# Query-key products on half of the array's rows: three 64-row products per head, two heads side by side

## The chip, the cores and the metric

The kernel runs on one core of a Trainium2 chip. The metric is the device time of one execution in microseconds (us); the comparison is between medians of several runs. TensorE is called PE in the rows of the profile (PEld is its weight load), VectorE is DVE, ScalarE is ACT, GpSimd is POOL, and SyncE, which here issues nearly all DMAs, is SP.

## The reference

One encoder block on x of shape (1, 1024, 1024) in float32. A single projection gives q, k, v and a gate z for two groups of eight heads of width 64. Group A is neighbourhood attention on a 16 by 64 grid of tokens (window 8 by 16, a learned bias per head and offset); group B is windowed attention (|i - j| <= 128) with rotary positions, four query heads per key head, and a sink logit. Both are gated and projected back:

```python
h = jnp.einsum('bsd,de->bse', x, w_in[layer])
q_a, k_a, v_a, z_a, q_b, k_b, v_b, z_b = jnp.split(h, SPLIT_POINTS, axis=-1)
y_a = neighborhood_attention(q_a, k_a, v_a, rel_pos_bias[layer])   # softmax(q k / 8 + bias) v
qb, kb = rotary(q_b, positions), rotary(k_b, positions)
y_b = windowed_gqa_with_sink(qb, kb, v_b, sink_logits[layer])      # softmax([q k / 8, sink]) v
mixed = jnp.concatenate([y_a * jax.nn.silu(z_a), y_b * jax.nn.silu(z_b)], axis=-1)
y = jnp.einsum('bse,ed->bsd', mixed, w_out[layer])
x = layer_norm(DEEPNORM_ALPHA * x + y, ln_gain[layer], ln_bias[layer])
```

## The kernel before

**Numbers in two halves.** Matmuls run in float16. Each operand is split into a high part and a low part (the remainder), and a product is the sum of three: high by high, low by high, high by low.

**Projection.** `project` makes one 128-column piece of h (two heads of q, k or z), in two halves of 512 tokens, each half being 24 matmuls of 512 columns (line 411) into one of two accumulator banks `ps_pj`. `evac` empties the bank: for z by a tanh and a product, for q and k by `split_q` and `split_k`, which write float16 high and low parts to tiles `qs` and `ks`. ScalarE makes the high part (lines 287, 289), VectorE or GpSimd the low part (293, 295). Before the change each head has a tile of its own. In a `q` tile one head's high part fills its own 64 partitions and its low part the other 64; in the `kh` tile the key's high part stands in both halves, where GpSimd copies it (`dup_`, line 325). So one matmul over 128 partitions (line 934) gives two of the three products at once, and one over 64 partitions (line 938) gives the third. For the group B keys `kb` GpSimd copies the low part as well, since heads of either half use it.

**Units.** The attention is 128 units of 128 queries by up to 384 keys: first 64 of group B (`p`, token block, head `j` of the pair), then 64 of group A (`p`, column block `b`, row `half`, head `j`). Four units make a quad, whose query-key products are issued together by `batch` and `stage_mm`. In group B the quad's units are (j=0, j=1) of one block and then of the next; in group A they are (half 0, j 0), (half 1, j 1), (half 0, j 1), (half 1, j 0).

**One unit's chain.** The product lands in one of five banks `ps_s`. VectorE adds the mask or the bias and takes the row minimum of the negated score (`stage_qk`, line 963, result in `sn` and `nm`). ScalarE takes the exponential (`stage_exp`, line 980), which goes back to the bank, or for the third unit of each quad to a tile `px`. `stage_tr` makes the high part on ScalarE (line 990) and the low part on VectorE (line 991, which frees the bank), and SyncE issues a transposing DMA (line 994). The product with v follows some nine steps later (`stage_pv`, line 1022, in the single bank `ps_t`), then the division by the sum (`stage_on`, lines 1027 and 1029), a transpose on PE (`stage_ot`, line 1040) and the product with the gate (lines 1046 and 1050), which reads `ps_t`.

**The order.** Everything from the projections to the last unit is issued in an order written out by hand: one step `i` per unit. In step `i` VectorE gets the minimum of unit `i`, then the low part of unit `i - 1`; ScalarE gets the high part of `i - 1`, then the exponential of `i`; when `i % 4 == 3` the next quad's products follow. Between these, `pump_to` feeds PE with matmuls of the list `fill`: the projections of `FILL`, and at the end the first terms of the output projection (`out_head`, matmuls of line 1170). Small jobs of the other engines wait in `queues` and are taken a few per step by `pop`. After the last step `final` issues the rest of the output projection and the layer norm; there a scheduler sets the order, and it may also put such work between the rows written by hand.

Of the kernel before, what the change touches and what calls it, by code (L numbers as in the profile page):

```python
# [18 lines left out]
GW = 64  # L19
# [34 lines left out]
EO = (4, 5, 6, 7, 0, 1, 2, 3)  # L54
# [9 lines left out]
NROW = (11, 12)  # L64
# [7 lines left out]
def hybrid_block(ctx, tc, xT, x, wt, wv, wo, bias, sink, gain, lbias, cos, sin, bmask, out):  # L72
# [203 lines left out]

    stks = {}

    def own(kind, p, j):
        if (kind, p, j) not in stks:  # L280
            stks[kind, p, j] = stk(kind)
        return stks[kind, p, j]

    def split_hl(h, l, src, scaled, eng):
        def hi():
            if scaled:
                nc.scalar.activation(h(), src, AF.Copy, scale=QSCALE)
            else:
                nc.scalar.copy(h(), src)

        def lo():
            if scaled:
                nc.vector.scalar_tensor_tensor(l(), src, QSCALE, h(), op0=ALU.mult, op1=ALU.subtract)
            else:
                (nc.gpsimd if eng == "pool" else nc.vector).tensor_sub(l(), src, h())

        return hi, lo

    def split_q(p, half, src, dep=None):
        sl = slice(512 * half, 512 * half + 512)  # L300
        ops = []
        prio = 0 if dep is None else 1
        eng = "pool" if dep and clock["step"] is not None else "dve"
        for j in range(2):
            a, o = slice(64 * j, 64 * j + 64), slice(64 - 64 * j, 128 - 64 * j)
            hi, lo = split_hl(lambda j=j, a=a: own("q", p, j)[a, sl], lambda j=j, o=o: own("q", p, j)[o, sl],
                              src[a], dep is None, eng)
            o1 = enq("act", hi, dep, prio=prio, after=28 if dep else 0)
            ops.append(enq(eng, lo, o1, prio=prio, after=32 if dep else 0))
            stk_ops.setdefault((p, j, half), []).append(ops[-1])  # L310
        return ops

    def split_k(p, half, src, dep=None):
        sl = slice(512 * half, 512 * half + 512)
        ops = []
        prio = 0 if dep is None else 1
        eng = "pool" if dep and clock["step"] is not None else "dve"
        for j in range(2):
            a, o = slice(64 * j, 64 * j + 64), slice(64 - 64 * j, 128 - 64 * j)
            hi, lo = split_hl(lambda j=j, a=a: own("kh", p, j)[a, sl], lambda j=j, a=a: own("kl", p, j)[a, sl],  # L320
                              src[a], dep is None, eng)

            def dup_(w, j=j, a=a, o=o):
                t = own(w, p, j)
                nc.gpsimd.tensor_copy(t[o, sl], t[a, sl])

            o1 = enq("act", hi, dep, prio=prio, after=28 if dep else 0)
            o2 = enq(eng, lo, o1, prio=prio, after=32 if dep else 0)
            ops.append(o2)
            dup = [enq("pool", lambda d=dup_: d("kh"), o1, after=32 if dep else 0)]  # L330
            dup.append(enq("pool", lambda d=dup_: d("kl"), o2, after=36) if dep else o2)
            stk_ops.setdefault((p, j, half), []).extend(dup)
        return ops

    def rope(ps, half):
        live = clock["step"] is not None
# [11 lines left out]
    def evac(name, half, ps):  # L348
        sl = slice(512 * half, 512 * half + 512)
        kind = name.rstrip("0123")  # L350
        p = int(name[-1]) if name[-1].isdigit() else 0
        n = ORDER.index(name)
        if kind in ("kb", "qb"):
            raw, o1, o5 = rope(ps, half)
            if kind == "kb":
                split_k("b", half, raw, o5)
            else:
                split_q(f"b{p}", half, raw, o5)
            return [o1]
        if kind == "k":  # L360
            return split_k(p, half, ps)
        if kind == "q":
            return split_q(p, half, ps)
# [7 lines left out]
        o = enq("act", lambda: nc.scalar.activation(zt[e][:, sl], ps, AF.Tanh, scale=half_inv), prio=0)  # L371
        o2 = enq("dve", lambda: nc.vector.scalar_tensor_tensor(
            zt[e][:, sl], zt[e][:, sl], 1.0, ps, op0=ALU.add, op1=ALU.mult), o, prio=0)
        stk_ops.setdefault(name, []).append(o2)
        return [o2]
# [7 lines left out]
    def new_group():  # L383
        if len(groups) >= 2:
            need(*groups[-2])
        return bank("pj")
# [527 lines left out]

    def qk_parts(u):
        g, p, j, t = u
        n, _c = geom(u)
        if g == "a":
            b, half = t
            q = stks["q", p, j][:, 512 * half + 128 * b:512 * half + 128 * b + 128]  # L920
            sl = [stks[w, p, j].rearrange("p (r c) -> p r c", c=GW)[
                :, 4 * half:4 * half + NROW[half], WIN0[b]:WIN0[b] + WINW[b]] for w in ("kh", "kl")]
            return NROW[half] * WINW[b], q, sl
        q = stks["q", f"b{p}", j][:, 128 * t:128 * t + 128]
        lo = max(t - 1, 0) * 128
        return n, q, [stks[w, "b", p // 2][:, lo:lo + n] for w in ("kh", "kl")]

    def stage_mm(us):
        for u in us:
            m, q, sl = qk_parts(u)  # L930
            ps = st[u, "ps"] = bank("s")
            if units.index(u) == WO_MAX + 4:
                wo_turn(ps)
            nc.tensor.matmul(ps[:, :m], q, sl[0], start=True, stop=False)  # L934
        for u in us:
            m, q, sl = qk_parts(u)
            a = slice(64 * u[2], 64 * u[2] + 64)
            nc.tensor.matmul(st[u, "ps"][:, :m], q[a], sl[1][a], start=False, stop=True)  # L938

    def stage_qk(u):  # L940
        g, p, j, t = u
# [231 lines left out]

    obank = {}

    def out_head(ts, es, tag):
        for t in ts:
            if tag == "pj":
                obank[t, 0] = new_group()
                groups.append([])  # L1180
            elif tag is not None:
                obank[t, 0] = bank(tag)
        for e in es:
            for t in ts:
                yield from out_mms(t, 0, obank[t, 0], [e])

    def final():
        actx.close()
# [116 lines left out]
        with tc.manual_schedule():  # L1305
# [11 lines left out]
    def batch(n):  # L1317
        us = units[n:n + 4]
        for u in us:
            if u[3] in (0, 4):  # L1320
                need(*stk_ops[f"b{u[1]}", u[2], u[3] // 4])
            if u[0] == "a" and n % 16 == 0:
                need(*stk_ops[u[1], u[2], 0], *stk_ops[u[1], u[2], 1])
        stage_mm(us)

    OT_AT = {(q, 0): (q - 3,) for q in range(3, 30)}
# [4 lines left out]
    for i in range(-LD, NU + LO):  # L1331
# [151 lines left out]
```

## Time and profile before

| | us |
|---|---|
| median of three runs (448.36 to 448.79) | 448.76 |
| the profiled execution: its own time | 448.48 |
| its span, from the first to the last instruction | 446.7 |
| PE busy, in the span | 437.7 |
| VectorE, ScalarE, GpSimd busy | 348.1, 310.9, 225.6 |

PE's granted clock is full (0.999). A busy share counts an instruction from its start to its modelled end; neighbouring matmuls overlap, so a matmul row of 379 ns is not the distance to the next one, and a short wait of PE can be hidden under the end of the matmul before it. Distances between starts show such waits.

### The profile page before, as it was taken

To read this page: it belongs to the slowest core of one execution; us is meant where nothing else is said; L and a number is where in the kernel's file an instruction comes from. 1 tells how busy PE (TensorE), PEld (TensorE's weight loads), DVE (VectorE), ACT (ScalarE), POOL (GpSimd) and SP (SyncE) were. 2 spreads that over 40 slices of the span, in tenths; PEclk is the share of its full clock that TensorE was granted. 3 is DMA by queue.
4 is the path that set the end of the run, shared out by engine and by line. 5 is a ranking of instruction groups with operands and counts; after the bars stand their busy time and mean duration, and the time that the engine had idled before them with its cause. 6 is when DMAs were issued, how large, how long until landed. Compare 5 with 4: busy or idle time off the path is not lost.

```text
span 446.7 us, 9468 instructions
## 1 busy us (share of the span) xinstructions
PE 437.7 (98%) x3275; PEld 241.9 (54%) x3275; DVE 348.1 (78%) x851; ACT 310.9 (70%) x721; POOL 225.6 (51%) x226
## 2 busy tenths in 40 slices
PE   9999999999999999999999999999999999999994
PEld 8987754444444545554545555555554554444442
DVE  5999948739978888888898798898877736179954
ACT  6798269766688889798898888888877866002211
POOL 0206734556837658768326529647563455005740
PEclk9999999999999999999999999999999999999999
DMA  8992078986837879577799879999999877101721
GB/s 299 302 361 70 21 248 261 306 272 257 287 91 179 132 165 179 131 131 159 154 170 197 177 168 197 199 200 202 217 213 197 154 185 320 48 0 70 251 79 70
DMA packets 133983, 81.76 MB, mean 183 GB/s; under 512 B 101296, under 2 KB 113328, under 8 KB 133680
## 3 DMA queue, kind: packets, MB, share of 16 engines
q1 hardware_dynamic: 133504, 80.67, 73.8%
q8 instruction: 25, 0.41, 0.4%
q10 hardware_dynamic: 432, 0.49, 0.4%
q14 instruction: 22, 0.18, 0.2%
HBM read 50.73 MB, written 9.96 MB: 136 GB/s over the span
## 4 chain that ended last, share of the span: by engine, by line
PE 69%; issue 9%; DVE 9%; ACT 6%; POOL 5%; DMA 1%; POOLq 0%; DVEq 0%; ACTq 0%
PE ps_pj L411 26%; PE ps_s L1170 11%; PE ps_t L1022 6%; PE ps_pj L1170 5%; PE ps_s L688 4%; PE ps_s L634 4%; PE ps_s L934 3%; POOL wl L217 2%; PE ps_t L1170 2%; PE ps_s L938 2%; ACT ps_s L980 2%; PE ps_pj L634 2%; PE ps_t L1040 2%; POOL wr L216 2%; DVE sn L963 2%
## 5 line engine op out<-in xcount | busy, mean ns | idle before, releaser
L411 PE MATMUL ps_pj<-xf,wh 128*128 128x512 f16 x672 | 204.0, 379 | 0.0
L411 PE MATMUL ps_pj<-xf,wl 128*128 128x512 f16 x336 | 127.6, 380 | 0.0
L411 PEld LDWEIGHTS <-wh 128*128 128x128 f16 x672 | 64.9, 98 | 72.6 <-issue 2.7
L980 ACT ACTIVATE ps_s<-sn,nm 128x385 f32<-128x385 f32 (+3 forms) x96 | 52.4, 546 | 19.9 <-DVE nm L963 18.7
L1170 PEld LDWEIGHTS <-m 128*128 128x128 f16 x408 | 38.8, 98 | 44.3 <-DVE eps L1191 1.2
L991 DVE SCALAR_TENSOR_TENSOR split<-ps_s,split 128x384 f16<-128x384 f32 (+2 forms) x96 | 49.1, 511 | 12.6 <-ACT split L990 12.2
L411 PEld LDWEIGHTS <-wl 128*128 128x128 f16 x336 | 32.8, 98 | 39.9 <-issue 6.2
L1170 PE MATMUL ps_s<-wo,m 128*128 128x512 f16 (+1 forms) x240 | 53.5, 374 | 0.0
L216 POOL TENSOR_SCALAR wr<-wr,wsc 128x512 f32<-128x512 f32 x26 | 22.0, 847 | 45.7 <-ACT wh L211 39.4
L990 ACT ACTIVATE split<-ps_s 128x384 f16<-128x384 f32 (+2 forms) x96 | 43.3, 451 | 2.0
L963 DVE CUSTOM_DVE_ANT_0 sn<-ps_s,bm,nsk 128x384 f32<-128x384 f32 (+1 forms) x64 | 40.6, 635 | 0.2
L1022 PEld LDWEIGHTS <-tr 128*128 128x128 f16 (+1 forms) x1104 | 36.6, 98 | 7.6
L963 DVE CUSTOM_DVE_ANT_0 sn<-ps_s,bias,sg 128x264 f32<-128x264 f32 (+1 forms) x64 | 35.0, 547 | 2.6 <-PE ps_s L938 1.9
L217 POOL TENSOR_TENSOR wl<-wr,wh 128x512 f16<-128x512 f32 x26 | 32.1, 1234 | 2.2
L1227 ACT ACTIVATE sd<-mv,eps 128x1 f32<-128x1 f32 x8 | 2.4, 294 | 43.7 <-DVE mv L1225 41.4
L908 POOL TENSOR_SCALAR bias<-bias,rsg 128x552 f32<-128x552 f32 (+1 forms) x24 | 18.7, 779 | 26.7 <-DMA bias<-in_bias 23.7
L1269 POOL TENSOR_TENSOR xr<-xr,gb 128x512 f32<-128x512 f32 x7 | 11.2, 1606 | 40.6 <-ACT xr L1266 40.6
L934 PE MATMUL ps_s<-ks,qs 128*128 128x384 f16 (+4 forms) x128 | 24.6, 306 | 1.3 <-DVE split L991 0.8
L991 DVE SCALAR_TENSOR_TENSOR split<-px,split 128x384 f16<-128x384 f32 (+2 forms) x32 | 23.2, 724 | 3.3 <-ACT split L990 3.2
L688 PEld LDWEIGHTS <-xf 128*128 128x128 f16 x216 | 21.0, 98 | 8.4 <-DVE xf L542 0.3
L1170 PE MATMUL ps_pj<-wo,m 128*128 128x512 f16 (+1 forms) x120 | 24.4, 347 | 0.0
L688 PE MATMUL ps_s<-wf,xf 128*128 128x320 f16 x144 | 23.8, 299 | 0.0
(216 smaller groups left out, 841.9 us busy)
## 6 DMA issues: line engine op xcount, KB each, us to landing
ws<-in_wt SPq DMA_DIRECT2D x15, 512.0 KB, 5.6
wr<-in_wt SPq DMA_DIRECT2D x26, 256.0 KB, 3.0
bias<-in_bias SPq DMA_DIRECT2D x16, 276.0 KB, 3.3
wor<-in_wo SPq DMA_DIRECT2D x16, 256.0 KB, 3.4
xr<-in_x SPq DMA_DIRECT2D x8, 512.0 KB, 7.6
xraw<-in_xT SPq DMA_DIRECT2D x15, 256.0 KB, 5.2
out<-xr SPq DMA_DIRECT2D x14, 256.0 KB, 2.0
bias<-in_bias SPq DMA_DIRECT2D x8, 368.0 KB, 4.4
```

The source lines that it names most:

```text
L216: nc.gpsimd.tensor_scalar(raw, raw, scale, 1.0, op0=ALU.mult, op1=ALU.mult)
L217: nc.gpsimd.tensor_sub(l, raw, h)
L411: nc.tensor.matmul(ps, a[:, k % 4, :], mv, start=(k == 0 and i == 0), stop=(k == KT - 1 and i == 2))
L634: nc.tensor.matmul(banks[t, a][:, :320], lh[k][:, 128 * t:128 * t + 128], rh[k][:, 320 * a:320 * a + 320], start=(k == 0 and i == 0), stop ...
L688: nc.tensor.matmul(ps[:, :320], lh[t // 4, k][:, 128 * (t % 4):128 * (t % 4) + 128], rh[k][:, 320 * a:320 * a + 320], start=(k == first an ...
L934: nc.tensor.matmul(ps[:, :m], q, sl[0], start=True, stop=False)
L963: nc.vector.tensor_tensor_reduce(sn[:, :m], ps[:, :m], bias_t, sg[:, c:c + 1], init, op0=ALU.add, op1=ALU.min, accum_out=nm)
L980: nc.scalar.activation(pt[:, :m], sn[:, :m], AF.Exp, bias=nm, scale=-1.0, accum_out=sm[:, k:k + 1])
L990: nc.scalar.activation(hl[:, :m, 0, :c], src, AF.Copy, scale=PSCALE)
L991: nc.vector.scalar_tensor_tensor(hl[:, :m, 1, :c], src, PSCALE, hl[:, :m, 0, :c], op0=ALU.mult, op1=ALU.subtract)
L1022: nc.tensor.matmul(ps[:, o:o + HD], a, b_, start=(i == 0), stop=(i == len(mms) - 1))
L1170: nc.tensor.matmul(ps, lh[:, ts], rh[:, cs], start=(e == EO[0] and i == 0), stop=(e == EO[-1] and i == 2))
```

## The change

- **Tiles.** `own` no longer keeps a tile per head. The high parts of both heads of a pair stand in one tile (head 0 in partitions 0 to 63, head 1 in 64 to 127), the low parts in another. `split_pair` writes each with one instruction over 128 partitions where `split_q` and `split_k` used two over 64. The copies on GpSimd stay for the group B keys alone (`split_kb`).
- **Products.** Each unit gets three matmuls over the 64 partitions of its head. They are issued in pairs, one head of each half in turn: (0, 1) and (2, 3) of the quad in group B, (0, 2) and (3, 1) in group A.
- **VectorE's order.** In step `i` it gets the minimum of unit `i + 1`. For the first unit of a quad this is right behind the quad's products, at the end of the step before.
- **Output projection.** The first twelve terms of (rows 0, second half) and (rows 1, second half) move from `final` to the end of `fill`, so they come after the last unit's transposes in the order written by hand.

```diff
-    def own(kind, p, j):
+    def own(kind, p):
...
+    def split_pair(kinds, p, half, src, dep=None):
         sl = slice(512 * half, 512 * half + 512)
-        ops = []
         prio = 0 if dep is None else 1
         eng = "pool" if dep and clock["step"] is not None else "dve"
+        hi, lo = split_hl(lambda: own(kinds[0], p)[:, sl], lambda: own(kinds[1], p)[:, sl], src, dep is None, eng)
+        o1 = enq("act", hi, dep, prio=prio, after=28 if dep else 0)
+        o2 = enq(eng, lo, o1, prio=prio, after=32 if dep else 0)
+        stk_ops.setdefault((p, half), []).append(o2)
+        return [o2]
...
     def qk_parts(u):
         g, p, j, t = u
-        n, _c = geom(u)
+        r = slice(64 * j, 64 * j + 64)
         if g == "a":
             b, half = t
+            n, o = NROW[half] * WINW[b], 512 * half + 128 * b
+            q = [stks[w, p][r, o:o + 128] for w in ("qh", "ql")]
+            k = [stks[w, p].rearrange("p (r c) -> p r c", c=GW)[
+                r, 4 * half:4 * half + NROW[half], WIN0[b]:WIN0[b] + WINW[b]] for w in ("kh", "kl")]
...
+        return n, ((q[0], k[0]), (q[1], k[0]), (q[0], k[1]))
 
     def stage_mm(us):
         for u in us:
-            m, q, sl = qk_parts(u)
             ps = st[u, "ps"] = bank("s")
             if units.index(u) == WO_MAX + 4:
                 wo_turn(ps)
-            nc.tensor.matmul(ps[:, :m], q, sl[0], start=True, stop=False)
-        for u in us:
-            m, q, sl = qk_parts(u)
-            a = slice(64 * u[2], 64 * u[2] + 64)
-            nc.tensor.matmul(st[u, "ps"][:, :m], q[a], sl[1][a], start=False, stop=True)
+        for pair in ((0, 1), (2, 3)) if us[0][0] == "b" else ((0, 2), (3, 1)):
+            for i in range(3):
+                for u in (us[c] for c in pair):
+                    m, parts = qk_parts(u)
+                    nc.tensor.matmul(st[u, "ps"][:, :m], *parts[i], start=i == 0, stop=i == 2)
...
-        for t, tag in ((0, "s"), (1, "s"), (2, "t")):
+        for t, tag in ((2, "t"),):
             obank[t, 1] = bank(tag)
             list(out_mms(t, 1, obank[t, 1], EO[:4]))
...
-                 out_head((3, 4), EO[:4], "s")))
+                 out_head((3, 4), EO[:4], "s"), out_head((0,), EO[:4], "s", 1), out_head((1,), EO[:4], "s", 1)))
...
         if i < NU:
             if i == 0:
                 batch(0)
-            stage_qk(units[i])
+                stage_qk(units[0])
+            if i % 4 != 3:
+                stage_qk(units[i + 1])
...
         if i % 4 == 3 and i + 1 < NU:
             pump_to(i + QK_AT)
             batch(i + 1)
+            stage_qk(units[i + 1])
```

On PE, the last quad (group A). Before: four matmuls over 128 partitions, of which the last two stand here, then four over 64; `ks_4442` and `ks_4471` are the doubled high parts of two heads' keys, `ks_4460` and `ks_4476` their low parts.

```order
L934 MATMUL ps_s_5346<-ks_4471,qs_4729 128x264
L934 LDWEIGHTS qs_4701
L934 MATMUL ps_s_5348<-ks_4442,qs_4701 128x288
L938 LDWEIGHTS qs_4701
L938 MATMUL ps_s_5342<-ks_4460,qs_4701 128x264
L938 LDWEIGHTS qs_4729
L938 MATMUL ps_s_5344<-ks_4476,qs_4729 128x288
L938 LDWEIGHTS qs_4729
L938 MATMUL ps_s_5346<-ks_4476,qs_4729 128x264
L938 LDWEIGHTS qs_4701
L938 MATMUL ps_s_5348<-ks_4460,qs_4701 128x288
```

The same quad now, its second pair of units: six matmuls over 64 partitions; `qs_4739` holds the high parts of both heads' queries, `qs_4763` the low ones, `ks_4483` and `ks_4507` the keys' high and low parts.

```order
L930 LDWEIGHTS qs_4739
L930 MATMUL ps_s_5397<-ks_4483,qs_4739 128x288
L930 LDWEIGHTS qs_4739
L930 MATMUL ps_s_5395<-ks_4483,qs_4739 128x288
L930 LDWEIGHTS qs_4763
L930 MATMUL ps_s_5397<-ks_4483,qs_4763 128x288
L930 LDWEIGHTS qs_4763
L930 MATMUL ps_s_5395<-ks_4483,qs_4763 128x288
L930 LDWEIGHTS qs_4739
L930 MATMUL ps_s_5397<-ks_4507,qs_4739 128x288
L930 LDWEIGHTS qs_4739
L930 MATMUL ps_s_5395<-ks_4507,qs_4739 128x288
```

The quad has twelve matmuls and weight loads where it had eight; three in a row go to one bank in turn with its neighbour's.

On VectorE, at a change of quads in group B (units 15 to 17; 963 and 955 are the minimum, 991 and 983 the low part). Before, each minimum is followed by the low part of the unit before it:

```order
L963 ISA sn0_1139,nm_1957<-ps_s_1941,bm_121,nsk_123,sg_108 128x256
L963 ISA nm_1957 128x1
L991 SCALAR_TENSOR_TENSOR split3_1136<-ps_s_1826,split3_1136 128x2x128
L958 COPY sn1_1140<-nsk_123 128x1
L963 ISA sn1_1140,nm_1975<-ps_s_1943,bm_121,nsk_123,sg_108 128x256
L963 ISA nm_1975 128x1
L991 SCALAR_TENSOR_TENSOR split4_1137<-ps_s_1941,split4_1137 128x2x128
```

and now:

```order
L955 ISA sn0_1139,nm_1968<-ps_s_1951,bm_121,nsk_123,sg_108 128x256
L955 ISA nm_1968 128x1
L950 COPY sn1_1140<-nsk_123 128x1
L955 ISA sn1_1140,nm_1973<-ps_s_1952,bm_121,nsk_123,sg_108 128x256
L955 ISA nm_1973 128x1
L983 SCALAR_TENSOR_TENSOR split3_1136<-ps_s_1828,split3_1136 128x2x128
L955 ISA sn0_1139,nm_1989<-ps_s_1953,bm_121,nsk_123,sg_108 128x384
L955 ISA nm_1989 128x1
L983 SCALAR_TENSOR_TENSOR split4_1137<-ps_s_1951,split4_1137 128x2x128
```

Two minima stand ahead of the low part of the last quad's last unit, and the minimum of a unit stands ahead of the low part of the unit two before it.

On PE, behind the last products with v. Before, the last transposes (1040) are followed at once by matmuls into the bank `ps_t` that they used:

```order
L1170 MATMUL ps_s_5476<-wo2_4294,m7_5240 128x512
L1040 MATMUL ps_t_1738<-identf_92,on_5531 128x128 x2
L1040 MATMUL ps_t_1738<-identf_92,on_5586 128x128 x2
L1170 LDWEIGHTS m4_4744
L1170 MATMUL ps_t_5703<-wo4_5450,m4_4744 128x512
```

and now by matmuls into another bank:

```order
L1162 MATMUL ps_s_5532<-wo2_4256,m7_5294 128x512
L1032 MATMUL ps_t_1745<-identf_92,on_5587 128x128 x2
L1032 MATMUL ps_t_1745<-identf_92,on_5642 128x128 x2
L1162 LDWEIGHTS m4_4784
L1162 MATMUL ps_s_5661<-wo4_5506,m4_4784 128x512
```

There are 24 of these ahead of the first one into `ps_t`. Before, the scheduler had put the same 24 further up: 14 between the last two products with v, ten behind the last one. So 23 matmuls stood between those two products, and now nine do.

More of the change, by code (lines that the diff above doesn't have):

```diff
@@ L277, in hybrid_block @@
     stks = {}
-    def own(kind, p, j):
-        if (kind, p, j) not in stks:
-            stks[kind, p, j] = stk(kind)
-        return stks[kind, p, j]
+    def own(kind, p):
+        if (kind, p) not in stks:
+            stks[kind, p] = stk(kind[0])
+        return stks[kind, p]
     def split_hl(h, l, src, scaled, eng):
@@ L304, in split_q, with split_kb @@
+    def split_kb(half, src, dep):
+        sl = slice(512 * half, 512 * half + 512)
         for j in range(2):
             a, o = slice(64 * j, 64 * j + 64), slice(64 - 64 * j, 128 - 64 * j)
[L306 to L333, printed above, removed]
+            hi, lo = split_hl(lambda j=j, a=a: own("kh", f"b{j}")[a, sl], lambda j=j, a=a: own("kl", f"b{j}")[a, sl],
+                              src[a], False, "dve")
@@ L335, in rope, with dup @@
+            def dup(w, j=j, a=a, o=o):
+                t = own(w, f"b{j}")
+                nc.gpsimd.tensor_copy(t[o, sl], t[a, sl])
+            enq("act", hi, after=28)
+            enq("dve", lo, after=32)
+            enq("pool", lambda d=dup: d("kh"), after=32)
+            enq("pool", lambda d=dup: d("kl"), after=36)
     def rope(ps, half):
@@ L1174, in hybrid_block, with out_head @@
     obank = {}
-    def out_head(ts, es, tag):
+    def out_head(ts, es, tag, a=0):
         for t in ts:
             if tag == "pj":
-                obank[t, 0] = new_group()
+                obank[t, a] = new_group()
                 groups.append([])
             elif tag is not None:
-                obank[t, 0] = bank(tag)
+                obank[t, a] = bank(tag)
         for e in es:
             for t in ts:
-                yield from out_mms(t, 0, obank[t, 0], [e])
+                yield from out_mms(t, a, obank[t, a], [e])
     def final():
@@ L1320, in batch @@
             if u[3] in (0, 4):
[L1321 removed]
+                need(*stk_ops[f"b{u[1]}", u[3] // 4])
             if u[0] == "a" and n % 16 == 0:
[L1323 removed]
+                need(*stk_ops[u[1], 0], *stk_ops[u[1], 1])
         stage_mm(us)
```

21 lines of the change are left out of this document (9 added, 12 removed).

## The prediction

> **What bounds the kernel now.** I read the page first, then who waited for whom on PE, then PE's instructions in order of time around the query-key products and the end.
>
> ```profile
> span 446.7 us, 9468 instructions
> PE 437.7 (98%) x3275; PEld 241.9 (54%) x3275; DVE 348.1 (78%) x851; ACT 310.9 (70%) x721; POOL 225.6 (51%) x226
> ```
>
> PE is the bound: 98% busy, no other engine over 78%. So work taken off VectorE, ScalarE or GpSimd shortens nothing by itself. The change can gain only where PE waits, or where PE's own rows get shorter. The list of PE's waits looks nearly empty:
>
> ```profile
> PE ps_t L1170 <- DVE eps L1191: 1.0, 1, 1.0
> PE ps_s L934 <- DVE split L991: 0.8, 2, 0.5
> PE ps_s L934 <- DVE nm L963: 0.2, 1, 0.2
> ```
>
> But a wait counts there only after the previous matmul's end, and a 384-column matmul runs 0.32 us while the next may start 0.16 us after it. The distance between starts tells more. The timeline of PE, start and length in us, first at two quads that nothing held (four products of 384 columns; then two of 256 and two of 384):
>
> ```profile
> 164.78 0.81 PE L934 MATMUL ps_s<-ks,qs 128*128 128x384 f16 x4
> 165.52 0.50 PE L938 MATMUL ps_s<-ks,qs 64*128 64x384 f16 x4
> 165.95 0.39 PE L411 MATMUL ps_pj<-xf,wl 128*128 128x512 f16 x1
> 166.18 0.38 PE L411 MATMUL ps_pj<-xf,wh 128*128 128x512 f16 x1
> ```
>
> ```profile
> 179.78 0.71 PE L934 MATMUL ps_s<-ks,qs 128*128 128x256 f16 x4
> 180.42 0.44 PE L938 MATMUL ps_s<-ks,qs 64*128 64x256 f16 x4
> ```
>
> and then at four that were held, in the same view:
>
> ```profile
> 135.07 0.49 PE L934 MATMUL ps_s<-ks,qs 128*128 128x384 f16 x2
> 135.75 0.79 PE L934 MATMUL ps_s<-ks,qs 128*128 128x384 f16 x2 [0.19 <-DVE nm L963]
> 136.48 0.50 PE L938 MATMUL ps_s<-ks,qs 64*128 64x384 f16 x4
> ```
>
> ```profile
> 142.33 0.60 PE L934 MATMUL ps_s<-ks,qs 128*128 128x384 f16 x3
> 143.23 0.27 PE L934 MATMUL ps_s<-ks,qs 128*128 128x256 f16 x1 [0.30 <-DVE split L991]
> 143.43 0.45 PE L938 MATMUL ps_s<-ks,qs 64*128 64x384 f16 x4
> ```
>
> ```profile
> 149.40 0.55 PE L934 MATMUL ps_s<-ks,qs 128*128 128x256 f16 x3
> 150.41 0.32 PE L934 MATMUL ps_s<-ks,qs 128*128 128x384 f16 x1 [0.46 <-DVE split L991]
> 150.66 0.45 PE L938 MATMUL ps_s<-ks,qs 64*128 64x256 f16 x4
> ```
>
> ```profile
> 209.92 1.17 PE L934 MATMUL ps_s<-ks,qs 128*128 128x256 f16 x4
> 211.02 0.45 PE L938 MATMUL ps_s<-ks,qs 64*128 64x256 f16 x4
> ```
>
> From the first 934 to the first 938 an undisturbed quad takes 0.74 us (all 384) or 0.64 (mixed). The held ones take 1.41, 1.10, 1.26 and 1.10: lost 0.67, 0.46, 0.62 and 0.46, together 2.2 us. What they wait for is a bank `ps_s`: the minimum or the low part of the quad before came late. The rest that PE loses before the layer norm is at the end of the units:
>
> ```profile
> 372.77 0.65 PE L1040 MATMUL ps_t<-identf,on 128*128 128x128 f32 x4
> 374.40 2.76 PE L1170 MATMUL ps_t<-wo,m 128*128 128x512 f16 x12 [0.97 <-DVE eps L1191]
> ```
>
> ```profile
> 373.46 0.88 DVE L1050 SCALAR_TENSOR_TENSOR z<-ps_t,zcol,z 128x256 f32<-128x256 f32 x2 [0.75 <-PE ps_t L1040]
> ```
>
> The 0.97 counts from the transposes' modelled end; a next matmul usually starts 0.07 to 0.16 before such an end (165.95 against 165.52 + 0.50; 166.18 against 165.95 + 0.39), so 1.1 us are lost. The next matmul writes `ps_t`, which the products with z read until 373.46 + 0.88 = 374.34 (the name `eps` stands for what follows on VectorE).
>
> **The change part by part.**
>
> *PE's products.* Before, a quad is four full-height matmuls, a switch to half height, and four half-height ones that run two at a time. That they do is in the rows: four 938 in 0.50 us, of which the last alone runs 0.32, so there were two starts, not four. Now it is six pairs. From the undisturbed quad: four 934 in 0.81 us are three distances of 0.16; the switch costs 0.74 - 4 x 0.16 = 0.10; first to second pair 0.50 - 0.32 = 0.18; last pair to the next matmul 165.95 - 165.52 - 0.18 = 0.25. New quad: 0.10 + 0.18 + 4 x 0.16 + 0.25 = 1.17 us. Old one: 165.95 - 164.78 = 1.17. So nothing, with as many switches as before. The doubt is the 0.18: if every later pair costs it, not the first alone, four pairs lose up to 0.02 each, 32 quads up to 2.6 us. I take 0, because the first full-height matmul behind the switch back shows the same excess (165.95 to 166.18 is 0.23, against 5.34 us for 24 in a row further down, (5.34 - 0.38) / 23 = 0.216 each): it belongs to a switch. Below nothing there is no room, since the same columns are streamed.
>
> *Weight loads.* A quad has twelve instead of eight. Their cover:
>
> ```profile
> 165.52 0.11 PEld L938 LDWEIGHTS <-qs 64*128 64x128 f16 x4 [0.32 <-issue]
> ```
>
> All four loads, the second pair's included, are done within 0.11 us, while the first pair streams for 0.16. So a load into rows whose matmul is running is hidden. The Trainium skill ("TensorE: Matmul & The Clock Gate", Part 3, The mechanism) says that a weight load overlaps running matmuls only when the row group differs; by that every later pair would stand behind its own load. The trace disagrees in this row, and I go by the row; the rule makes the slow rival below.
>
> *Evacuation of q and k.* The group rows:
>
> ```profile
> L293 DVE SCALAR_TENSOR_TENSOR qs<-ps_pj,qs 64x512 f16<-64x512 f32 x16 | 11.0, 689 | 1.7 <-ACT qs L287 1.2
> L293 DVE SCALAR_TENSOR_TENSOR ks<-ps_pj,ks 64x512 f16<-64x512 f32 x16 | 11.0, 685 | 1.2 <-ACT ks L287 0.8
> L287 ACT ACTIVATE ks<-ps_pj 64x512 f16<-64x512 f32 x16 | 9.4, 586 | 1.5 <-DVE ks L293 1.1 <-PE ps_pj L411 0.3
> L372 DVE SCALAR_TENSOR_TENSOR z<-z,ps_pj 128x512 f32<-128x512 f32 x10 | 6.8, 682 | 0.3 <-ACT z L371 0.2
> L325 POOL COPY ks<-ks 64x512 f16<-64x512 f16 x24 | 16.8, 698 | 4.4 <-DVE ks L295 1.8 <-ACT ks L287 1.3
> ```
>
> 128 partitions take as long as 64 (682 ns for z). So VectorE loses 16 of 32 rows, 11 us; ScalarE 16 of about 0.59, 9 us, and half of the rotary queries' casts; GpSimd 16 of 24 copies, 11 us. On the path that sets the end this is worth nothing but the stalls. It reaches them: VectorE's first minimum stood behind two rotary splits that are halved,
>
> ```profile
> 119.47 2.63 DVE L295 TENSOR_TENSOR qs<-rp_raw,qs 64x512 f16<-64x512 f32 x2
> 124.02 1.39 DVE L295 TENSOR_TENSOR qs<-rp_raw,qs 64x512 f16<-64x512 f32 x2
> ```
>
> so it starts (2.63 + 1.39) / 2 = 2.0 us sooner, as much as the 1.75 us that the first three held quads lose.
>
> *The minimum a step sooner.*
>
> ```profile
> L980 ACT ACTIVATE ps_s<-sn,nm 128x385 f32<-128x385 f32 (+3 forms) x96 | 52.4, 546 | 19.9 <-DVE nm L963 18.7 <-DVE wog L1094 0.5
> L963 DVE CUSTOM_DVE_ANT_0 sn<-ps_s,bias,sg 128x264 f32<-128x264 f32 (+1 forms) x64 | 35.0, 547 | 2.6 <-PE ps_s L938 1.9
> ```
>
> ScalarE waited 18.7 us for minima; most of that goes. The price: on VectorE the low part that frees a bank stands behind one minimum more, 0.6 us, and at a change of quads behind two that wait for PE's products. Queued there are the low part of the last unit, its transposing DMA on SP, and the evacuations. The bias is needed 1.5 to 2 us sooner; the second row shows no wait for GpSimd, which makes it. A minimum now also waits for the exponential two units before it, since there are two `sn` tiles, 0.55 us at most. Against the held quads: gains 2.0 us by the sooner start and the shorter chain, loses 0.6 by the order. I take 2.1 of the 2.2 us as gone; the ends are 2.3 (a further quad lost 0.1) and 0.8.
>
> *Output terms behind the last transposes.* 24 matmuls take 5.3 us (below), VectorE's two products 0.9: the wait of 1.1 us is covered and goes. What is late next is the last product with v. 14 matmuls that stood before it are gone, 14 x 0.216 = 3.0 us, so PE comes to it at 366.19 - 3.0 = 363.2.
>
> ```profile
> 366.19 1.21 PE L1022 MATMUL ps_t<-va,tr 96*128 96x64 f16 x36
> 408.08 5.34 PE L1170 MATMUL ps_s<-wo,m 128*128 128x512 f16 x24
> ```
>
> ```profile
> 353.38 9.18 SPq L994 DMA_TRANSPOSE tr<-split  x6
> DMA to landing us min/median/max: 2.7/2.9/5.0
> ```
>
> Its fourth unit comes 0.8 us later, at 364.0. Six transposing DMAs stood back to back on SP until 362.56, the last from about 361.3, landing 2.9 later at 364.2: a new wait of 0.2 us if they stay. They should come sooner with the minima. I take 0, with 0.3 as the bad end.
>
> *Sum.* -2.1 - 1.1 + 0 + 0 = -3.2 us on the profiled execution's own 448.48, so 445.3. The median of the runs shown is 0.28 above that execution; I predict 445.5.
>
> **The rivals.**
>
> 1. *The held quads stay* (chance 0.15). VectorE does not get ahead, since the low part stands behind one minimum more and its order, not its load, is what holds. For it: in the later quads it also waits for PE's transposes, and that does not change. Against: the start 2.0 us sooner and ScalarE's 18.7 us. Then only the end gains: 448.76 - 1.1 = 447.6.
> 2. *The end gives nothing* (0.10). PE reaches the last products with v 3.0 us sooner and waits there instead; SP is full at that place (six in 9.18 us). It costs all of the 1.1 only if the last DMA comes 0.9 us later than before. Then 448.76 - 2.1 = 446.7.
> 3. *Later pairs stand behind their weight loads* (0.07, the slow side). Each of a quad's four later pairs that the old quad did not have would wait for part of a load. The load row gives about 0.1 us as the full price: 32 x 4 x 0.1 = 12.8 us, so 448.76 - 3.2 + 12.8 = 458. It turns the sign from 3.2 / 128 = 0.025 us per pair, a quarter of a load. Against it: the pairs that can be seen cost 0.02 at most.
> 4. *Nothing comes of it* (0.05): the waits move elsewhere, as to a bank `ps_pj` whose evacuation is queued behind a waiting minimum; 448.0 to 449.5.
>
> **How the numbers follow.** The forecast has 0.63. Its own range goes from 444.8 (the fastest run, 448.36, less 2.3 + 1.1, and 0.2 for half the spread of the runs) to 447.2 (the bad ends: 448.76 - 0.8 - 1.1 + 0.3). With rivals 1 and 2 the range is 444.8 to 447.6, which leaves out some 0.15. A measurement of this kernel tells about 0.2%, 0.9 us, from no change. Faster by more than that, under 447.9: 0.63 + 0.12 + 0.10 = 0.85. Within it: a weak case of rival 1 and half of rival 4, 0.07. Slower: rival 3 and some of 4, 0.08.
>
> **What would show it.** Right: a quad of 384 takes 1.07 us from its first product to the next projection, with the switch's 0.10 ahead of the first product; twelve products in six starts; no `ps_s` wait at the quads near 135 to 150 and 210; no wait at the transposes; ScalarE's wait for `nm` well under 10 us. Wrong: starts of later pairs 0.2 us apart or more (rival 3); marks of `split` or `nm` on PE's product rows (rival 1); a wait for a DMA on the last rows of 1022 (rival 2).

## The result, and the profile after

The changed kernel takes 445.25 us (median of four runs, 444.64 to 445.36) against 448.63 for the kernel before in the same comparison: ratio 0.9922, 95% interval 0.9905 to 0.994. The profiled execution took 445.36 us with a span of 443.6. That is 3.1 us less than before, by own time as by span. In the changed file the lines named below have moved: 934 and 938 are now 930, 411 is 401, 963 is 955, 980 is 972, 991 is 983, 1022 is 1014, 1040 is 1032, 1046 and 1050 are 1038 and 1042, 1170 is 1162.

The page first: span, then the busy time of each engine.

```profile
span 443.6 us, 9636 instructions
PE 436.6 (98%) x3403; PEld 242.0 (55%) x3403; DVE 334.5 (75%) x833; ACT 293.7 (66%) x697; POOL 210.6 (47%) x204
```

VectorE is 13.6 us lighter, ScalarE 17.2, GpSimd 15.0, and PE is still 98% busy. PE's list of waits is all that is left of it:

```profile
PE ps_t L1244 <- ACT dg L1243: 1.5, 1, 1.5
PE ps_t L440 <- PEq L1467: 0.8, 1, 0.8
```

No wait for `ps_s` and none behind the transposes: these two rows stand in the list of before too, in the layer norm and at the start. The timeline of PE at the places that were held near 135, 142, 149 and 210 us:

```profile
134.42 0.59 PE L401 MATMUL ps_pj<-xf,wh 128*128 128x512 f16 x2
134.95 1.15 PE L930 MATMUL ps_s<-ks,qs 64*128 64x384 f16 x12
136.03 0.39 PE L401 MATMUL ps_pj<-xf,wl 128*128 128x512 f16 x1
...
141.54 0.99 PE L930 MATMUL ps_s<-ks,qs 64*128 64x384 f16 x12
...
148.15 0.99 PE L930 MATMUL ps_s<-ks,qs 64*128 64x256 f16 x12
...
207.91 0.99 PE L930 MATMUL ps_s<-ks,qs 64*128 64x256 f16 x12
```

One row now holds a quad's twelve products. A quad of 384 columns lasts 1.15, one of mixed width (256 and 384) 0.99, here and in the rest of group B: nothing is held. From the first product to the next projection are 136.03 - 134.95 = 1.08 us, and the first product comes 0.10 later behind the last projection than another projection would (that one starts at 134.42 + 0.59 - 0.38 = 134.63, and 134.95 - 134.63 is 0.32 against 0.216). Together 1.18, as before. The end of the units:

```profile
360.87 1.22 PE L1014 MATMUL ps_t<-va,tr 96*128 96x64 f16 x36
...
365.29 0.66 PE L1032 MATMUL ps_t<-identf,on 128*128 128x128 f32 x4
365.79 5.34 PE L1162 MATMUL ps_s<-wo,m 128*128 128x512 f16 x24
370.96 2.32 PE L1162 MATMUL ps_t<-wo,m 128*128 128x512 f16 x10
```

```profile
365.99 0.88 DVE L1042 SCALAR_TENSOR_TENSOR z<-ps_t,zcol,z 128x256 f32<-128x256 f32 x2 [0.75 <-PE ps_t L1032]
```

PE goes from the last transpose straight into 24 output terms; VectorE is done with `ps_t` at 366.87, and PE wants it at 370.96. The gap of 1.24 us between the starts of the last transpose and the next term is gone. One loss is new in this execution, at a product with v in group A, which takes 1.45 us where 1.22 is usual (the group row names a DMA, with 0.2 us):

```profile
275.93 1.45 PE L1014 MATMUL ps_t<-va,tr 96*128 96x64 f16 x36
```

```profile
L1014 PEld LDWEIGHTS <-tr 128*128 128x128 f16 (+1 forms) x1104 | 36.6, 98 | 7.7 <-DMA tr<-split 0.2
```

In the traces of the ten other kernels below, the same product takes 1.21 to 1.22, so this wait is not shown to belong to the change. The sum of the profile is: held quads -2.35 (the forecast's four, 2.2, and two small ones near 195 and 202 us, 0.04 and 0.10), the end -1.13, this DMA +0.23, the rest of the program +0.15.

### The profile page after: what moved, and what is told of

The parts are those of the page before. It is cut to its first block, busy times and chain, and to the rows that moved or that the text cites. A ratio compares the mean times of both kernels' runs of the same rounds, so it can differ in the third digit from the quotient of the medians.

```text
span 443.6 us, 9636 instructions
## 1 busy us (share of the span) xinstructions
PE 436.6 (98%) x3403; PEld 242.0 (55%) x3403; DVE 334.5 (75%) x833; ACT 293.7 (66%) x697; POOL 210.6 (47%) x204
## 4 chain that ended last, share of the span: by engine, by line
PE 97%; DMA 1%; DVE 0%; ACT 0%; issue 0%; ACTq 0%
PE ps_pj L401 49%; PE ps_s L1162 11%; PE ps_t L1014 7%; PE ps_s L930 7%; PE ps_pj L1162 5%; PE ps_s L678 4%; PE ps_s L624 4%; PE ps_t L1162 2%; PE ps_t L1032 2%; PE ps_pj L624 2%; PE ps_pj L678 1%; DMA tr<-split 1%; PE ps_t L440 1%; PE ps_t L678 1%; PE ps_t L1244 0%; DVE xr L1239 0%
## 5 line engine op out<-in xcount | busy, mean ns | idle before, releaser
L1162 PEld LDWEIGHTS <-m 128*128 128x128 f16 x408 | 38.9, 98 | 43.2 <-issue 0.4
L955 DVE CUSTOM_DVE_ANT_0 sn<-ps_s,bias,sg 128x264 f32<-128x264 f32 (+1 forms) x64 | 34.7, 546 | 11.6 <-PE ps_s L930 10.1
L930 PE MATMUL ps_s<-ks,qs 64*128 64x384 f16 (+4 forms) x384 | 33.0, 305 | 0.0
L930 PEld LDWEIGHTS <-qs 64*128 64x128 f16 x384 | 16.1, 94 | 19.1 <-issue 13.4
L216 POOL TENSOR_SCALAR ws<-ws,wsc 128x512 f32<-128x512 f32 x16 | 11.4, 710 | 28.2 <-ACT wh L211 28.2
L983 DVE SCALAR_TENSOR_TENSOR split<-px,split 128x384 f16<-128x384 f32 (+2 forms) x32 | 21.7, 679 | 3.4 <-ACT split L982 3.4
```

Source lines behind the costliest of these rows:

```text
L216: nc.gpsimd.tensor_scalar(raw, raw, scale, 1.0, op0=ALU.mult, op1=ALU.mult)
L930: nc.tensor.matmul(st[u, "ps"][:, :m], *parts[i], start=i == 0, stop=i == 2)
L955: nc.vector.tensor_tensor_reduce(sn[:, :m], ps[:, :m], bias_t, sg[:, c:c + 1], init, op0=ALU.add, op1=ALU.min, accum_out=nm)
L983: nc.vector.scalar_tensor_tensor(hl[:, :m, 1, :c], src, PSCALE, hl[:, :m, 0, :c], op0=ALU.mult, op1=ALU.subtract)
L1162: nc.tensor.matmul(ps, lh[:, ts], rh[:, cs], start=(e == EO[0] and i == 0), stop=(e == EO[-1] and i == 2))
```

## The experiments

The change has three separable parts: the tiles with their products and evacuations, the minimum a step sooner, and the output terms. The forecast put one sum of 2.1 us on the first two together and did not say which of them is needed. That is what the runs were chosen for. "Lost in quads" below is the time from a quad's first product to the next projection, less what a quad of the same shapes takes undisturbed, summed over all 32, in the one profiled execution of each kernel; before it is 2.35 us. Executions also differ by what happens before the first quad (it starts between 122.1 and 123.8 us), so the quads are a finer gauge than the time.

### One part alone

*The minimum alone*, in the kernel before:

```diff
         if i < NU:
             if i == 0:
                 batch(0)
-            stage_qk(units[i])
+                stage_qk(units[0])
+            if i % 4 != 3:
+                stage_qk(units[i + 1])
...
             batch(i + 1)
+            stage_qk(units[i + 1])
```

> The kernel before with one part of the change: the minimum a step sooner; tiles, products and output terms as before. If the order of VectorE is what frees the banks sooner, the held quads at 135 to 210 us lose nothing any more: about 2.2 us less, 446.4. If instead the lighter evacuation and the sooner start made the difference, the low parts are only later by one minimum: 448.6 to 449.2, and the first three quads are still held.

Measured: 446.32 us (446.13 to 446.87), ratio 0.9959, interval 0.9945 to 0.9972. The timeline of PE in this kernel, in the form of before (four products over 128 rows, four over 64), at three quads that still lose something, and its wait at the end:

```profile
128.66 0.94 PE L934 MATMUL ps_s<-ks,qs 128*128 128x384 f16 x4
129.53 0.50 PE L938 MATMUL ps_s<-ks,qs 64*128 64x384 f16 x4
135.15 1.00 PE L934 MATMUL ps_s<-ks,qs 128*128 128x384 f16 x4
136.08 0.50 PE L938 MATMUL ps_s<-ks,qs 64*128 64x384 f16 x4
...
148.54 0.84 PE L934 MATMUL ps_s<-ks,qs 128*128 128x256 f16 x4
149.31 0.44 PE L938 MATMUL ps_s<-ks,qs 64*128 64x256 f16 x4
```

```profile
PE ps_t L1170 <- DVE eps L1191: 1.0, 1, 1.0
```

From the first 934 to the first 938 are 0.87, 0.93 and 0.77 instead of 0.74, 0.74 and 0.64: 0.45 us lost in all. The new order alone recovers 1.9 of the 2.35, and the end stays as it was.

*The output terms alone*, in the kernel before (the same edit of `out_head`, `final` and `fill` as in the change):

```diff
-        for t, tag in ((0, "s"), (1, "s"), (2, "t")):
+        for t, tag in ((2, "t"),):
...
-                 out_head((3, 4), EO[:4], "s")))
+                 out_head((3, 4), EO[:4], "s"), out_head((0,), EO[:4], "s", 1), out_head((1,), EO[:4], "s", 1)))
```

> The kernel before with the 24 output terms behind the last transposes, nothing else. Theory: the 1.1 us wait for ps_t is covered, 447.5, and no wait at the last products with v above 0.3 us. Rival: PE waits there for the transposing DMAs instead, 448.6.

Measured: 447.09 us (446.7 to 447.86), ratio 0.9978, interval 0.9969 to 0.9986: -1.1. The held quads are all there; the wait behind the transposes is gone:

```profile
135.82 0.79 PE L934 MATMUL ps_s<-ks,qs 128*128 128x384 f16 x2 [0.19 <-DVE nm L963]
...
367.70 0.66 PE L1040 MATMUL ps_t<-identf,on 128*128 128x128 f32 x4
368.20 5.34 PE L1170 MATMUL ps_s<-wo,m 128*128 128x512 f16 x24
```

*The tiles alone*: the changed kernel with the old step of the minimum (first edit: two places) and the old place of the output terms (second edit: the two lines here, and `out_head` as it was).

```diff
         if i < NU:
             if i == 0:
                 batch(0)
-                stage_qk(units[0])
-            if i % 4 != 3:
-                stage_qk(units[i + 1])
+            stage_qk(units[i])
...
             batch(i + 1)
-            stage_qk(units[i + 1])
...
-        for t, tag in ((2, "t"),):
+        for t, tag in ((0, "s"), (1, "s"), (2, "t")):
...
-                 out_head((3, 4), EO[:4], "s"), out_head((0,), EO[:4], "s", 1), out_head((1,), EO[:4], "s", 1)))
+                 out_head((3, 4), EO[:4], "s")))
```

> The kernel before with the new tiles and the six pairs of products, the minimum at its old step, output terms as before. If VectorE's order is what counts, the start 2 us sooner frees the first three held quads in part and the one at 210 stays: about 1 us less, 447.6. If the lighter evacuation does it all, 2.2 us less: 446.4. If pairs cost PE more than before it is slower than 448.6; the quads' length says so directly.

Measured: 446.24 us (445.69 to 447.48), ratio 0.9959, interval 0.9944 to 0.9974. That is "lighter work", not "order". PE's timeline has one held quad, 1.34 long where 0.99 is undisturbed:

```profile
149.38 1.34 PE L930 MATMUL ps_s<-ks,qs 64*128 64x256 f16 x12
```

This execution took 447.48 us, the longest of the six, although it loses only 0.36 in quads: its first quad starts at 123.76, 1.1 us later than in the kernel before.

So the minimum alone and the tiles alone each recover some 2 us. The next runs show that it is the same 2 us.

### One part left out

Each part taken back out of the whole change. Without the minimum (the first edit of the diff above, alone):

> The whole change with the minimum back at its old step. If VectorE's order is what counts: about 446.5, the quads near 149 and 210 us held again. If the tiles do it all: 445.3.

Measured: 445.47 us (444.76 to 445.63), ratio 0.9934, interval 0.9921 to 0.9946. Lost in quads: 0.34, at the same single quad (its row is shown further down). The step forward is not needed once the tiles are there.

Without the output terms (the second edit alone):

> The whole change with the 24 output terms back where the scheduler puts them. Theory: the 1.1 us wait for ps_t is back, 446.4. Rival (the end gives nothing): 445.3.

Measured: 446.09 us (445.99 to 447.25), ratio 0.9962, interval 0.9948 to 0.9975. PE waits behind the transposes as before:

```profile
370.03 0.65 PE L1032 MATMUL ps_t<-identf,on 128*128 128x128 f32 x4
371.65 2.76 PE L1162 MATMUL ps_t<-wo,m 128*128 128x512 f16 x12 [0.97 <-DVE eps L1183]
```

Without the tiles, which is the kernel before with the first two edits, the minimum and the output terms:

> Everything but the tiles and pairs: minimum a step sooner and output terms moved, old products. If the order does it: 445.3, as with the whole change. If the lighter work is needed: 447.5, the end's 1.1 us alone.

Measured: 445.27 us (444.75 to 445.71), ratio 0.9934, interval 0.9921 to 0.9947. Lost in quads 0.45, as with the minimum alone. The part of the change with the most lines in it can be left away with no loss that these times could tell: the intervals of this ratio and of the whole change's (0.9922, 0.9905 to 0.994) overlap, and the quads show 0.45 us.

### What in the tiles does it

The tiles bring three things: half as many evacuations, sixteen copies fewer on GpSimd, and another order of products. The whole change with q and k written by two instructions over 64 partitions again:

```diff
-        hi, lo = split_hl(lambda: own(kinds[0], p)[:, sl], lambda: own(kinds[1], p)[:, sl], src, dep is None, eng)
-        o1 = enq("act", hi, dep, prio=prio, after=28 if dep else 0)
-        o2 = enq(eng, lo, o1, prio=prio, after=32 if dep else 0)
-        stk_ops.setdefault((p, half), []).append(o2)
-        return [o2]
+        ops = []
+        for j in range(2):
+            a = slice(64 * j, 64 * j + 64)
+            hi, lo = split_hl(lambda a=a: own(kinds[0], p)[a, sl], lambda a=a: own(kinds[1], p)[a, sl], src[a],
+                              dep is None, eng)
+            o1 = enq("act", hi, dep, prio=prio, after=28 if dep else 0)
+            ops.append(enq(eng, lo, o1, prio=prio, after=32 if dep else 0))
+        stk_ops.setdefault((p, half), []).extend(ops)
+        return ops
```

> The whole change, but q and k of group A and the rotary q are split with two instructions over 64 partitions each instead of one over 128: the new layout with the old count of evacuations on ScalarE, VectorE and GpSimd (the copies stay away). If the saved evacuations are off the path, 445.3 to 445.6. If they are what freed the held quads, 446 to 447.5 with waits near 135 to 150.

Measured: 445.09 us (444.6 to 445.34), ratio 0.9926, interval 0.9914 to 0.9939; lost in quads 0.08. VectorE is 12.3 us busier than with the whole change (346.8), ScalarE 12.9 (306.6), GpSimd 6.6 (217.2), and it cost nothing. And the same with the minimum at its old step as well:

> The new tiles, the six pairs and the output terms as in the whole change, but the minimum at its old step and q and k written with two instructions over 64 partitions, as before. With the one-instruction writes and the old step one quad was held, by 0.34 us, and the time was 445.47. Theory 'lighter VectorE': the tiles remove the held quads because VectorE starts on the units about 2 us sooner; with two writes that head start is gone, so three or four of the quads near 136, 143, 150 and 210 us wait for their banks again, 1.1 to 2.2 us in all: 446.4 to 447.1. Theory 'pairs': the order of the new products (or the sixteen copies gone from GpSimd) does it, not the evacuations: at most one quad held, 445.3 to 445.7.

Measured: 447.25 us (446.1 to 448.48), ratio 0.9977, interval 0.9965 to 0.999. "Lighter VectorE", just above the upper end of what it gave, 447.1 (the runs of this kernel spread more than the others'). PE's timeline, the quad near 136 us and the following ones, and the one at 210:

```profile
135.36 1.57 PE L934 MATMUL ps_s<-ks,qs 64*128 64x384 f16 x12
142.38 1.40 PE L934 MATMUL ps_s<-ks,qs 64*128 64x384 f16 x12
149.40 0.66 PE L934 MATMUL ps_s<-ks,qs 64*128 64x256 f16 x7
150.47 0.64 PE L934 MATMUL ps_s<-ks,qs 64*128 64x384 f16 x5 [0.41 <-DVE split L987]
...
209.88 1.27 PE L934 MATMUL ps_s<-ks,qs 64*128 64x256 f16 x12
```

The same quads with the one-instruction writes (no minimum either):

```profile
135.05 1.15 PE L930 MATMUL ps_s<-ks,qs 64*128 64x384 f16 x12
141.64 0.99 PE L930 MATMUL ps_s<-ks,qs 64*128 64x384 f16 x12
148.25 1.33 PE L930 MATMUL ps_s<-ks,qs 64*128 64x256 f16 x12
```

The four quads of before are held again, by 0.42, 0.41, 0.72 (150.47 + 0.64 - 149.40 is 1.71, for 0.99) and 0.28: 1.8 us, for 0.34. Between the two kernels stands the evacuation alone. For the three quads before 150 us, 1.2 of the 1.5 us between them, it can act only through the start of the units: between the first minimum and 150 us both kernels have the same evacuations of q and k, none on VectorE, two casts on ScalarE (1.2 us) and two splits on GpSimd (2.5 and 2.6 us). For the quad at 210 us (0.28), later evacuations lie in between, and whether they count is not shown. VectorE's timeline, with two writes and with one, from the last rotary splits to the first minimum:

```profile
119.56 2.74 DVE L295 TENSOR_TENSOR qs<-rp_raw,qs 64x512 f16<-64x512 f32 x2
124.10 1.38 DVE L295 TENSOR_TENSOR qs<-rp_raw,qs 64x512 f16<-64x512 f32 x2
126.16 0.54 DVE L959 CUSTOM_DVE_ANT_0 sn<-ps_s,bm,nsk 128x256 f32<-128x256 f32 x1
```

```profile
119.25 1.64 DVE L295 TENSOR_TENSOR qs<-rp_raw,qs 128x512 f16<-128x512 f32 x1
123.16 0.68 DVE L295 TENSOR_TENSOR qs<-rp_raw,qs 128x512 f16<-128x512 f32 x1
124.42 0.53 DVE L955 CUSTOM_DVE_ANT_0 sn<-ps_s,bm,nsk 128x256 f32<-128x256 f32 x1
```

The splits shrink from 4.12 to 2.32 us and the first minimum comes 1.7 us sooner, or 1.4 counted from the start of the first quad, which moves a little from run to run. Set side by side, with the first minimum counted in that way (the medians are from separate comparisons, in which the kernel before took 448.2 to 448.6):

| kernel | minimum sooner | one-instruction writes | first minimum, us | lost in quads, us | median, us |
|---|---|---|---|---|---|
| before | no | no | 3.4 | 2.35 | 448.2 to 448.6 |
| two writes, no minimum* | no | no | 3.2 | 1.84 | 447.25 |
| without minimum* | no | yes | 1.8 | 0.34 | 445.47 |
| without tiles* | yes | no | 3.4 | 0.45 | 445.27 |
| two writes* | yes | no | 3.2 | 0.08 | 445.09 |
| whole change* | yes | yes | 1.8 | 0 | 445.25 |

(* with the output terms moved, worth 1.1.) Either the sooner start or the sooner order brings the loss under 0.5 us; with both, nothing is left to gain. The pairs of products and the copies that went are together worth at most the difference of the first two rows, 0.5, and of the fourth and fifth, 0.4; which of the two gives it was not tried.

### The order of the products

Does the alternation of the two heads matter? Two more forms of `stage_mm`. In the first the three products of a unit stand in a row:

```diff
         for pair in ((0, 1), (2, 3)) if us[0][0] == "b" else ((0, 2), (3, 1)):
-            for i in range(3):
-                for u in (us[c] for c in pair):
+            for u in (us[c] for c in pair):
+                for i in range(3):
```

> The whole change, but the three products of a unit in a row instead of in turn with its neighbour's. PE starts matmuls in their order, so only the last product of one unit can run beside the first of the next: nine starts in place of six, 3 x 0.146 us x 32 quads = 14 us more, about 459. If PE lets the other half's products overtake, no change: 445.3. This prices what side by side is worth.

Measured: 445.74 us (two runs, 445.16 and 446.31), ratio 0.9943, interval 0.9925 to 0.9961. The 459 that was expected first was wrong by 13 us; the other case that it names, 445.3, is what came. The timeline has a quad as long as ever:

```profile
135.67 1.16 PE L930 MATMUL ps_s<-ks,qs 64*128 64x384 f16 x12
```

Nine starts about 0.16 us apart, the expectation's count if matmuls start in their order, would make it about 1.6. So the first product of the second unit passes two of the first unit that wait ahead of it, and runs in the other half of the rows. The program that is built has the products in the order of the edit, so it is not the scheduler that turned them round. In the second form all six products of head 0 stand ahead of the six of head 1:

```diff
-        for pair in ((0, 1), (2, 3)) if us[0][0] == "b" else ((0, 2), (3, 1)):
-            for i in range(3):
-                for u in (us[c] for c in pair):
+        for u in sorted(us, key=lambda u: u[2]):
+            if True:
+                for i in range(3):
```

> The whole change, but the six products of one head's two units stand ahead of the six of the other head: a product and the one that runs beside it are now six places apart. When the three products of a unit stood in a row the two halves still ran side by side, the second 10 ns behind the first (3 to 4 ns where they alternate), 1.088 us a quad of 384 columns instead of 1.081. Theory 'each half of the rows has its own line': the order between the halves does not matter at any distance, the second starts some 20 ns behind the first, a quad takes 1.08 to 1.12 us and the run about 445.3 to 446.5. Theory 'PE looks a few products ahead': six places are too far; the halves overlap only in part and a quad takes 1.4 to 1.9 us, 32 of them 10 to 26 us more, 455 to 470.

Measured: 453.75 us, one run, beside 448.55 for the kernel before. The timeline:

```profile
128.38 1.49 PE L930 MATMUL ps_s<-ks,qs 64*128 64x384 f16 x12
...
148.97 1.22 PE L930 MATMUL ps_s<-ks,qs 64*128 64x256 f16 x12
```

"A few ahead" holds in kind: 0.34 us more on each quad of 384, 9.4 over all 32 quads (some narrower ones lose less), and 453.75 where it gave 455 to 470. The starts of one 384-column quad in the trace, in ns from its first product, show how many:

| order | starts |
|---|---|
| heads alternate | 0, 4, 174, 177, 336, 339, 499, 502, 661, 664, 824, 827 |
| unit by unit | 0, 10, 173, 183, 336, 346, 498, 508, 661, 671, 823, 833 |
| head by head | 0, 172, 335, 343, 497, 516, 660, 678, 822, 841, 1003, 1166 |

In the last row two starts at the front and two at the back have no partner. Sorted by their spacing, one head starts at 0, 172, 335, 497, 660 and 822, the other at 343, 516, 678, 841, 1003 and 1166: its first product starts 8 ns after the third of the head in front, when three still wait ahead of it, and not when four do. In all 32 quads of this execution it is so (8 to 9 ns). Each product has its weight load with it in the program; whether the matmuls or the loads set this limit is not shown.

## Why the prediction was right, and where it was not

The forecast of 445.5 us holds (445.25), and so do the two terms that made its sum.

- *Held quads, -2.1.* They lost 2.35 by starts and lose nothing now. The sum is right, but the working behind it is loose: "gains 2.0 us by the sooner start and the shorter chain, loses 0.6 by the order" treats the order as a price. The runs show it as a second sufficient cause. The tiles alone (start 1.6 sooner, counted from the first quad) recover 2.0, the order alone recovers 1.9, both together 2.35; the gains do not add up. What the order can cost, a low part behind one minimum more, is at most the 0.45 that the kernels with the order alone still lose, and with the tiles it is nothing. The bad end of this term, 0.8, was therefore too pessimistic. The 2.1 was taken, not added up from sizes, so that it came so near is in part luck.
- *The end, -1.1.* Measured -1.13 in the starts, -1.1 alone and about -0.8 when left out of the whole (446.09 against 445.25, medians of two comparisons; the trace of that kernel has the full gap of 1.24 again). The cover is ample: `ps_t` is free 4 us before PE wants it.
- *PE's products, 0.* Right to 0.01 us: 0.10 for the switch, 173 ns from the first pair to the second, 162 to 163 between later ones. The doubtful 0.18 belonged to the switch. Rival 3, and with it the rule of the Trainium skill ("TensorE: Matmul & The Clock Gate", Part 3, The mechanism) that a load overlaps only matmuls of another row group, is refuted for these rows: later pairs stream without a gap, with a load between any two products of a half. (The same section also lets a load go ahead of running matmuls into a background weight buffer, and that would fit them.)
- *The evacuations, nothing by themselves.* Shown by putting them back: no difference, as long as the minimum comes sooner. With the old order they are worth 1.5 us (1.84 against 0.34 lost), 1.2 of it through the start.
- *The last product with v.* PE came to it at 360.87, and it runs 1.22 us, as undisturbed. Rival 2 did not occur there in this execution, but it is real in a mild form. In the kernels that keep the output terms at their old place the last product takes 1.21 to 1.22. With the terms moved it takes 1.27 (output terms alone), 1.31 (without the minimum) and 1.49 (unit by unit, where the profile names the transposing DMA, 0.22); in five others, the changed kernel among them, it is not held. The forecast's 0.2, and 0.3 as the bad end, was the right size for a wait that comes in some executions.
- *"ScalarE waited 18.7 us for minima; most of that goes": wrong.* So was the sign to look for, "well under 10 us". ScalarE's waits for minima after, in the kernel before, in the kernel with the minimum alone, and in the changed kernel without it:

```profile
ACT ps_s L972 <- DVE nm L955: 21.0, 29, 1.4
```

```profile
ACT ps_s L980 <- DVE nm L963: 18.7, 32, 1.8
...
ACT px L980 <- DVE nm L963: 7.0, 14, 1.0
```

```profile
ACT ps_s L980 <- DVE nm L963: 12.4, 14, 1.8
```

```profile
ACT px L972 <- DVE nm L955: 23.1, 25, 1.7
ACT ps_s L972 <- DVE nm L955: 15.2, 28, 1.0
```

The order does what was said of it, 25.7 to 12.4 us (the forecast overlooked the second row of before). But the tiles without it raise the wait to 38.3 (also with nothing else: 22.7 + 15.6). It is the evacuations that do this: with two writes and the old order it is 23.8, with one 38.3; with the new order 10.1 and 21.0. The reading is that PE sets the pace, so an engine that is given less to do waits longer at the next thing that PE paces.

VectorE's list after:

```profile
DVE z L1042 <- PE ps_t L1032: 19.3, 15, 2.2
DVE z L1038 <- PE ps_t L1032: 18.3, 15, 1.7
DVE sn L955 <- PE ps_s L930: 13.2, 20, 1.6
```

The first two were 24.5 us together before, and are 38.9 in the changed kernel without the minimum: lighter work, longer waits, as on ScalarE. The third was 1.9 before (in the group row that the prediction shows), and it comes from the order: with the minimum alone, and in the changed kernel without it, it is

```profile
DVE sn L963 <- PE ps_s L938: 10.9, 15, 1.4
```

```profile
DVE sn L955 <- PE ps_s L930: 1.7, 3, 0.7
```

A minimum that stands right behind its products waits for them. In return VectorE stands less before the low part, for ScalarE's high part, before and with the minimum alone:

```profile
DVE split L991 <- ACT split L990: 15.3, 35, 0.9
```

```profile
DVE split L991 <- ACT split L990: 4.6, 12, 1.1
```

The sum did not rest on the 18.7 us, so the time came out right all the same; the low chance of rival 1 did rest on them in part.

## What to carry to other kernels

When one engine is 98% busy, list the distances between its starts and ask of each gap how early its releaser would have to be. Two edits that each make the same releaser early enough are worth one of them, so take a part out as well as putting it in alone before counting it: here a few lines of order did what the new layout did. The wait of an engine that is not the bound is no gauge of progress; here ScalarE's grew when its work shrank.

## What the runs showed of the hardware

- Products on the two halves of the array's rows need not alternate in the program. With three in a row on one half, the other half starts 10 ns later and runs beside it (1.088 us a quad instead of 1.081). With six in a row it starts, in the one execution of that kernel, only when no more than three are left waiting, and a quad takes 1.42 us. The Trainium skill ("TensorE: Matmul & The Clock Gate", Part 3, The mechanism) has matmuls start and end strictly in program order; the starts here do not agree with that, since in that order the first form would have had nine starts and a quad about 1.6 us (an estimate: eight distances of 0.163 and the 0.255 to the next projection).
- Going from 128 rows to 64 costs about 0.10 us here, and so does going back: the first product comes 0.312 us behind the last projection where another projection would come at 0.216, and the last pair to the next projection is 0.255 us where pairs are 0.163 apart. The first product behind a switch is listed with 333 ns, the others with 322 (384 columns).
